# Twenty-four conditioning columns of the first attention layer made on TensorE, and a third raw weight buffer

## The chip, the cores and the metric

The kernel runs on one core of a Trainium2 chip. The metric is device time of one execution in microseconds (us). The engines are TensorE (PE in the rows, PEld for its weight loads), VectorE (DVE), ScalarE (ACT), GpSimd (POOL) and SyncE (SP, which here only issues transfers).

## The reference, cut to what matters

Two transformer layers over 512 tokens of width 1024, in float32. Each layer first makes six conditioning vectors of 1024 values from a vector `c`, uses three of them around the attention and three around the MLP:

```python
c_act = jax.nn.silu(c)
for l in range(DEPTH):                       # DEPTH = 2
    ada = c_act @ ada_w[l] + ada_b[l]        # 1024 x 6144 weights for each layer
    sh1, sc1, g1, sh2, sc2, g2 = jnp.split(ada, 6, axis=-1)
    h = modulate(x, sh1, sc1)                # x * (1 + sc1) + sh1
    y = even_mixer(h, ...) if l % 2 == 0 else diff_mixer(h, ...)
    x = layer_norm(ALPHA * x + (1.0 + g1) * y, ln_g[l, 0], ln_b[l, 0])
    h = modulate(x, sh2, sc2)
    y = sq_relu_mlp(h, mlp_w1[l], mlp_w2[l]) # square(relu(h @ w1)) @ w2, inner width 4096
    x = layer_norm(ALPHA * x + (1.0 + g2) * y, ln_g[l, 1], ln_b[l, 1])
```

`even_mixer` projects `h` once and feeds two attentions: NSA (compressed, selected and windowed keys, 8 heads) and DSA (an indexer scores the keys, the 256 best of each query are kept, 8 heads). Their joined output goes through one output projection.

## The kernel before

**Columns.** The 6144 conditioning values of a layer are 48 columns of 128 (`adac[:, l, m]`). In layer 0, columns 0 to 15 are the shift and scale ahead of the attention, 16 to 23 (`ada2`) the gate `g1`, 24 to 39 (`adaE`) the shift and scale ahead of the MLP, and 40 to 47 the gate `g2`. Each column needs 512 KB of weights. There are two ways to make one:

- on VectorE, GpSimd and ScalarE: the weights lie with one output value per partition, and are multiplied with `cact`, a row of 1024 numbers that stands in every partition. Columns 0 to 15, and three of the others (the table `ax`), take one VectorE instruction that multiplies and sums (L250). The other 21 of columns 16 to 39 take a GpSimd multiplication in place (L247) and a ScalarE pass that sums (L248). `ada_bias` (L407) then adds the bias to eight columns at a time.
- on TensorE, two columns at a time (`ada_pair`, L416): eight matmuls of the raw weights against the vector `ccol` (L422) into a PSUM bank, a ScalarE copy (L425), two small matmuls (L427) that turn the result into two columns, and a VectorE add that takes the bias along (L428). Columns 40 to 47 of layer 0 and all 48 of layer 1 are made so. Of a pair, the first raw buffer stays occupied (`held`) until the matmuls of the pair have read both.

**Stream.** All weights come in one list in program order, by the queue of SP, into raw buffers of 512 KB (`issue`, L134). `process` then prepares each in list order: a column, or a split of a weight chunk into a high part (`hi`, ScalarE cast, L265) and a low part (`lo`, a subtraction on VectorE or GpSimd, L266), which TensorE takes in three matmuls a product (L350 to L352). The output weights (`eo`) are also multiplied by a gate row (`grow`, L262). Two raw buffers stand for the whole kernel; four "early" ones are taken only at the start and up to the NSA, four others only in the tails and MLPs.

**Order.** In `even`, a start phase makes columns 0 to 15 and the first eight weight chunks. Then come input projections (`iq`, `ks`, `kw` and others, L350 to L352), the indexer's scores (L504, L505, the same lines as all scores) with L1159 to L1164 behind them, and the latent keys (L1095 to L1113: an RMS norm, whose L384 to L398 are a square root made by VectorE, and transposes). `n0` is the first chunk of the query projections. The table `ord` sets the order of the loads there; `a` is a column of `ada2`. In the NSA units that follow, `st.pump(2)` takes up to two items from the stream in each; the `adaE` columns and the chunks `eo` are among them, and the gate row is made once `ada2` is done (`gate_row`). The DSA units (about 240 to 370 us) take in the last columns and `eo4` to `eo7`. `gtile` (L537) loads a bias tile, on SP's queue as the weights are.

All engines run their instructions in the order written; the code's order on each engine comes from a scheduler.

Of the kernel before, what the change touches and what calls it, by code (L numbers as in the profile page):

```python
# [9 lines left out]
F32 = mybir.dt.float32  # L10
F32R = mybir.dt.float32r
I32 = mybir.dt.int32
AF = mybir.ActivationFunctionType
ALU = mybir.AluOpType
# [14 lines left out]
def f32(ap):  # L29
# [4 lines left out]
PLAN = {'se': ((0, 1, 0, 0, 1, 0, 0), (0, 1, 1, 0, 0, 1, 0)),  # L34
 'sl': ((1, 1, 0, 1, 0, 1, 0), (1, 0, 0, 0, 0, 0, 0)),
 'ax': ((0, 19), (0, 36), (0, 38)),
 'sc': ('eo2', 'eo3', 'eo4', 'eo5', 'eo7', 'oo5', 'z018'),
 'lo': {'n0': 0,
        'dq2': 1,
        'dq3': 0,  # L40
        'dq0': 1,
        'qk70': 0,
# [28 lines left out]
 'fz': (1, 2, 3, 0, 4, 5),  # L71
 'ord': ('iq', 'a', 'ks', 'n0', 'a', 'kw', 'a', 'a', 'a', 'a', 'kc', 'vc', 0, 'a', 1, 2, 3, 'n1', 4, 5, 'a', 6, 7,
         'n2', 'n3'),
# [33 lines left out]
class Stream:  # L107
# [130 lines left out]
    def prepare(self, it):  # L238
        k, nc = self.k, self.k.nc
        n = it.n  # L240
        raw = it.raw[0][:, :n]
        if it.ada is not None:
            l, m = it.ada
            if not k.ada_pe(l, m):
                acc = k.adac[:, l, m:m + 1]
                if bool(16 <= m < 48) != ((l, m) in PLAN["ax"]):
                    nc.gpsimd.tensor_tensor(out=raw, in0=raw, in1=k.cact, op=ALU.mult)  # L247
                    nc.scalar.activation(out=raw, in_=raw, func=AF.Copy, scale=0.5, accum_out=acc)  # L248
                else:
                    nc.vector.scalar_tensor_tensor(out=raw, in0=raw, scalar=0.5, in1=k.cact, op0=ALU.mult,  # L250
                                                   op1=ALU.mult, accum_out=acc)
            elif m % 2:
                k.ada_pair(l, m - 1, self.held.raw[0], raw)
# [73 lines left out]
class Trunk:  # L327
# [76 lines left out]

    def ada_bias(self, l, sp):
        sl = slice(8 * sp, 8 * sp + 8)
        self.nc.vector.tensor_add(out=self.adac[:, l, sl], in0=self.adac[:, l, sl], in1=self.adab[:, l, sl])  # L407

    def ada_pe(self, l, m):

        return l > 0 or m >= 40

    def ada_src(self, l, m):
        return self.a["ada_p"][8 + m if l else m - 40] if self.ada_pe(l, m) else self.a["ada_w"][m]

# [127 lines left out]
    def start(self):  # L543
        nc, a, C = self.nc, self.a, self.C

        c, t = self.cond, self.s4()
        self.cact = C.tile([128, 1024], F32, name="cact")
        self.one = C.tile([128, 1], F32, name="one")
# [488 lines left out]
    def even(self):  # L1037
        nc, a, sm, R, B, st, I = self.nc, self.a, self.sm, self.R, self.B, self.st, self.I
# [36 lines left out]
        iq = []  # L1075
# [246 lines left out]
        for slot in range(end):  # L1322
# [36 lines left out]
            if n >= 2 and (0, 0) not in self.gate and (I["ada2", 7].done or n == 14):  # L1359
                st.get(I["ada2", 7])  # L1360
                self.ada_bias(0, 2)
                self.gate_row(0, 0)
# [109 lines left out]
        for m in (3, 4):  # L1472
            st.get(I["adaE", 8 * m + 7])
            self.ada_bias(0, m)
        return od, [I["eo", k] for k in range(4, 8)]
# [341 lines left out]
    def run(self):  # L1817
        tc = self.tc
        with tc.tile_pool(name="c", bufs=1) as self.C, tc.tile_pool(name="sm", bufs=1) as self.sm, \
# [3 lines left out]
            st = self.st  # L1823
            for s in range(2):
                st.raws.append((self.W.tile([128, 1024], F32, name=f"raw{s}"), 1 << 30))
# [34 lines left out]
def layout(i):  # L1860
    c = np.ascontiguousarray
    i = {k: np.asarray(v) for k, v in i.items()}
    f = {}
# [9 lines left out]
    f["cT"] = c(i["c"].reshape(8, 128).T)  # L1873
    f["ada_w"] = c(i["ada_w"][0, :, :5120].reshape(1024, 40, 128).transpose(1, 2, 0))
    p = i["ada_w"].reshape(2, 2, 4, 128, 24, 256).transpose(0, 4, 1, 3, 2, 5).reshape(96, 128, 1024)
    f["ada_p"] = c(p[40:])
    f["ada_b"] = c(i["ada_b"].reshape(2, 48, 128).transpose(2, 0, 1))
# [52 lines left out]
```

## Time and profile before

| | |
|---|---|
| time before, median of 3 runs | 1440.21 us (1439.06 to 1440.84) |
| profiled execution, its own time | 1441.48 us |
| its span, first to last instruction | 1439.4 us |
| mean granted TensorE clock | 0.968 |
| TensorE busy | 1338.4 us, 93% |
| VectorE busy | 1141.7 us, 79% |
| ScalarE busy | 659.8 us, 46% |
| GpSimd busy | 579.8 us, 40% |

The shares are means over stages with different limits: the start and even attention (0 to some 370 us), the first MLP, the second attention and the second MLP. TensorE's busy time counts a matmul from its start to a modelled end, so that matmuls that follow each other at some distance also look busy without a gap. The granted clock is 1.00 at 2.4 GHz and 0.50 at 1.2 GHz.

### The profile page before, as it was taken

The numbers are of one execution on the slowest core, as the hardware profiler recorded it, in microseconds if no ns is written. First come the engines' busy times: TensorE is split into PE (matmuls) and PEld (weight loads), VectorE is DVE, ScalarE is ACT, GpSimd is POOL, SyncE is SP. The second block draws the span as 40 slices with busy tenths as digits, with TensorE's granted clock in tenths as the row PEclk, the third lists the DMA queues.
The fourth block names the chain that finished last, engine by engine and source line by source line (L and its number), as shares of the span: only waits on it lengthen the run. The fifth ranks groups of instructions, "written<-read, shape, count | busy, mean of one in ns | idle before, by whom it ended". The sixth has DMA issues, their size and how long they took to land.

```text
span 1439.4 us, 22546 instructions
## 1 busy us (share of the span) xinstructions
PE 1338.4 (93%) x8286; PEld 1123.1 (78%) x8286; DVE 1141.7 (79%) x2186; ACT 659.8 (46%) x1412; POOL 579.8 (40%) x432
## 2 busy tenths in 40 slices
PE   6979799998899999999999799999979899999985
PEld 4868676676589888888887687887769789999974
DVE  7778979667569778877789925788976997888898
ACT  3555465746365423333332536776565443333321
POOL 1423577626432444444453721124164533122234
PEclk9989999899999999999999999999989999999997
DMA  9834323313731554544542442332450233323311
GB/s 353 288 116 142 116 89 118 119 58 118 263 117 46 175 191 162 183 169 161 191 161 94 144 164 88 103 103 76 152 163 6 91 100 118 106 72 117 117 59 59
DMA packets 58657, 189.52 MB, mean 132 GB/s; under 512 B 7794, under 2 KB 8498, under 8 KB 58548
## 3 DMA queue, kind: packets, MB, share of 16 engines
q1 hardware_dynamic: 55840, 184.67, 38.0%
q10 hardware_dynamic: 2708, 3.42, 0.7%
q8 instruction: 65, 1.06, 0.3%
q14 instruction: 44, 0.36, 0.1%
HBM read 178.42 MB, written 9.64 MB: 131 GB/s over the span
## 4 chain that ended last, share of the span: by engine, by line
PE 70%; DVE 19%; DMA 4%; issue 3%; ACT 2%; POOL 1%; DVEq 0%; SPq 0%; ACTq 0%; POOLq 0%
PE ps_mm L350 9%; PE ps_mm L351 9%; PE ps_mm L352 9%; PE ps_o L350 4%; PE ps_o L351 4%; PE ps_o L352 4%; PE ps_s L351 3%; PE ps_s L350 3%; PE ps_s L352 3%; PE ps_t L350 2%; PE ps_t L352 2%; PE ps_t L351 2%; PE ps_t L1486 2%; PE ps_s L504 2%; DVE u L738 2%
## 5 line engine op out<-in xcount | busy, mean ns | idle before, releaser
L350 PE MATMUL ps_mm<-hT,b 128*128 128x256 f32 (+1 forms) x560 | 188.9, 339 | 16.9 <-ACT b L265 13.2
L351 PE MATMUL ps_mm<-hT,b 128*128 128x256 f32 (+1 forms) x560 | 188.5, 337 | 5.2 <-DVE hT L724 5.1
L352 PE MATMUL ps_mm<-hT,b 128*128 128x256 f32 (+1 forms) x560 | 187.8, 336 | 1.8 <-DVE b L220 1.8
L350 PEld LDWEIGHTS ps_mm<-hT,b 128*128 128x128 f32 x560 | 107.6, 192 | 31.9 <-ACT b L265 13.2
L351 PEld LDWEIGHTS ps_mm<-hT,b 128*128 128x128 f32 x560 | 107.8, 193 | 17.8 <-DVE hT L724 5.6
L220 POOL TENSOR_TENSOR b<-s,b 128x512 fp32r<-128x512 f32 x33 | 46.6, 1415 | 184.6 <-ACT b L219 181.2
L517 ACT ACTIVATE z<-z,st 128x128 f32<-128x128 f32 (+3 forms) x160 | 89.3, 559 | 67.2 <-DVE st L514 61.3
L903 POOL TENSOR_TENSOR ot<-z,ot 128x512 fp32r<-128x512 f32 x39 | 61.3, 1573 | 142.0 <-ACT ot L902 128.4
L352 PEld LDWEIGHTS ps_mm<-hT,b 128*128 128x128 f32 x560 | 107.5, 192 | 11.4 <-DVE b L220 2.0
L350 PE MATMUL ps_o<-b,ot 128*128 128x512 f32 x251 | 101.2, 403 | 3.9 <-ACT b L265 2.2
L351 PE MATMUL ps_o<-b,ot 128*128 128x512 f32 x251 | 99.5, 397 | 3.0 <-DVE b L266 3.0
L738 DVE TENSOR_TENSOR u<-ps_o,u 128x512 f32<-128x512 f32 x121 | 82.4, 681 | 21.6 <-PE ps_o L352 21.2
L352 PE MATMUL ps_o<-b,ot 128*128 128x512 f32 x251 | 98.8, 394 | 0.0
L514 DVE CUSTOM_DVE_ANT_0 z<-ps_s,g 128x128 f32<-128x128 f32 (+3 forms) x160 | 75.0, 484 | 25.8 <-PE ps_s L505 23.6
L265 ACT CAST b<-raw 128x1024 fp32r<-128x1024 f32 (+1 forms) x62 | 64.5, 1043 | 65.9 <-issue 16.7
L266 DVE TENSOR_TENSOR b<-s,b 128x1024 fp32r<-128x1024 f32 x47 | 70.4, 1501 | 18.3 <-ACT b L265 17.9
L265 ACT CAST b<-s 128x1024 fp32r<-128x1024 f32 x47 | 49.1, 1049 | 77.6 <-DMA s<-mlp_w 18.9
L266 DVE TENSOR_TENSOR b<-raw,b 128x1024 fp32r<-128x1024 f32 (+1 forms) x42 | 56.7, 1349 | 33.1 <-ACT b L265 32.9
L350 PE MATMUL ps_s<-b,ot 128*128 128x512 f32 x181 | 72.4, 400 | 0.0
L738 DVE TENSOR_TENSOR u<-ps_s,u 128x512 f32<-128x512 f32 x87 | 59.3, 682 | 15.9 <-PE ps_s L352 15.6
L351 PE MATMUL ps_s<-b,ot 128*128 128x512 f32 x181 | 71.7, 396 | 0.0
L352 PE MATMUL ps_s<-b,ot 128*128 128x512 f32 x181 | 71.4, 394 | 0.0
(472 smaller groups left out, 4244.1 us busy)
## 6 DMA issues: line engine op xcount, KB each, us to landing
s<-mlp_w SPq DMA_DIRECT2D x55, 512.0 KB
s<-ada_p SPq DMA_DIRECT2D x39, 512.0 KB
s<-mlp_wp SPq DMA_DIRECT2D x33, 512.0 KB
raw<-ada_w SPq DMA_DIRECT2D x23, 512.0 KB
raw<-mlp_w SPq DMA_DIRECT2D x21, 512.0 KB
raw<-mlp_wp SPq DMA_DIRECT2D x19, 512.0 KB
early<-ada_w SPq DMA_DIRECT2D x17, 512.0 KB
raw<-ada_p SPq DMA_DIRECT2D x17, 512.0 KB
```

The lines of the kernel that those rows point to most:

```text
L220: (nc.gpsimd if PLAN["sl"][it.l][n] else nc.vector).tensor_tensor(out=lo, in0=src, in1=f32(hi), op=ALU.subtract)
L265: nc.scalar.copy(out=hi.cols(c.start, w), in_=raw[:, c])
L266: getattr(nc, ("vector", "gpsimd")[PLAN["lo"][it.name]] if it.name in PLAN["lo"] else k.lo_engine).tensor_sub(out=lo.cols(c.start, w), in0 ...
L350: mm(ps, lhsT=l[0], rhs=r[0], start=start, stop=False)
L351: mm(ps, lhsT=l[0], rhs=r[1], start=False, stop=False)
L352: mm(ps, lhsT=l[1], rhs=r[0], start=False, stop=stop)
L504: mm(ps, lhsT=q[:, qs], rhs=k[0][:, ks], start=start, stop=False)
L514: i = nc.vector.tensor_tensor_reduce(out=z[:, :w], in0=ps, in1=bias, scale=-1.0, scalar=3e38, op0=ALU.add, op1=ALU.min, accum_out=st[:, m: ...
L517: j = nc.scalar.activation(out=z[:, :w], in_=z[:, :w], func=AF.Exp, scale=-1.0, bias=st[:, m:m + 1], accum_out=st[:, 2 + m:3 + m])
L738: self.nc.vector.tensor_add(out=u[:, sl], in0=ps, in1=u[:, sl])
L903: (nc.gpsimd if PLAN["hl"][l][f % 2] else nc.vector).tensor_tensor(out=hl[:, c0:c1], in0=r[:, c0:c1], in1=f32(hh[:, c0:c1]), op=ALU.subtract)
L1486: self.nc.tensor.transpose(t[:, 128 * j:128 * j + 128], z[:, 128 * j:128 * j + 128], self.ident)
```

## The change

All 24 columns 16 to 39 of layer 0 are made by `ada_pair`, so that L247, L248, the table `ax` and `ada_bias` go. The weights of these columns come in the layout of the pairs (`ada_p`); 512 KB a column as before. The row `cact`, which only columns 0 to 15 need now, shares its room with the gate row (`grow`), and a third raw buffer for the whole kernel takes the room that this gives. The table `ord` has `a` at other places: `iq`, then two columns, then `ks` and `n0`, where `iq`, one column, `ks`, `n0` and one column stood.

```diff
- 'ax': ((0, 19), (0, 36), (0, 38)),
...
- 'ord': ('iq', 'a', 'ks', 'n0', 'a', 'kw', 'a', 'a', 'a', 'a', 'kc', 'vc', 0, 'a', 1, 2, 3, 'n1', 4, 5, 'a', 6, 7,
+ 'ord': ('iq', 'a', 'a', 'ks', 'n0', 'kw', 'a', 'a', 'a', 'a', 'kc', 'vc', 0, 'a', 'a', 1, 2, 3, 'n1', 4, 5, 6, 7,
          'n2', 'n3'),
...
             if not k.ada_pe(l, m):
-                acc = k.adac[:, l, m:m + 1]
-                if bool(16 <= m < 48) != ((l, m) in PLAN["ax"]):
-                    nc.gpsimd.tensor_tensor(out=raw, in0=raw, in1=k.cact, op=ALU.mult)
-                    nc.scalar.activation(out=raw, in_=raw, func=AF.Copy, scale=0.5, accum_out=acc)
-                else:
-                    nc.vector.scalar_tensor_tensor(out=raw, in0=raw, scalar=0.5, in1=k.cact, op0=ALU.mult,
-                                                   op1=ALU.mult, accum_out=acc)
+                nc.vector.scalar_tensor_tensor(out=raw, in0=raw, scalar=0.5, in1=k.cact, op0=ALU.mult,
+                                               op1=ALU.mult, accum_out=k.adac[:, l, m:m + 1])
...
-    def ada_bias(self, l, sp):
...
     def ada_pe(self, l, m):

-        return l > 0 or m >= 40
+        return l > 0 or m >= 16
...
-        self.cact = C.tile([128, 1024], F32, name="cact")
+        self.cact = self.B.tile([128, 1024], F32, tag="grow", bufs=1, name="cact")
...
-            for s in range(2):
+            for s in range(3):
                 st.raws.append((self.W.tile([128, 1024], F32, name=f"raw{s}"), 1 << 30))
```

The scheduler places what the change adds. In the changed kernel's code all later lines lie some ten lower: L412, L415, L417 and L418 are the pair's L422, L425, L427 and L428, L344 to L346 are L350 to L352, L494 and L495 are L504 and L505, L1103 is L1113, and L260 is L266.

TensorE before, from the end of the `ks` projection (chunk `b_85`, `b_86`) to the first transposes of the latent keys:

```order
L352 MATMUL ps_mm<-hT,b_86 128x512
L504 MATMUL ps_s<-q,ot 128x512
L505 MATMUL ps_s<-q,ot 128x512
L504 MATMUL ps_s<-q,ot 128x512
L505 MATMUL ps_s<-q,ot 128x512
L1113 MATMUL ps_t<-ident,ot 128x128 x3
L504 MATMUL ps_s<-q,ot 128x512
L505 MATMUL ps_s<-q,ot 128x512
L1113 MATMUL ps_t<-ident,ot 128x128
```

TensorE of the changed kernel at the same place, where `ks` is chunk `b_86`, `b_87`; one pair lies ahead of `ks`, behind `iq`:

```order
L412 MATMUL ps_mm<-raw_75,ccol 32x256 x4
L412 MATMUL ps_mm<-raw_76,ccol 32x256 x4
L344 MATMUL ps_mm<-hT,b_86 128x512
L345 MATMUL ps_mm<-hT,b_86 128x512
L346 MATMUL ps_mm<-hT,b_87 128x512
L1103 MATMUL ps_t<-ident,ot 128x128 x4
L417 MATMUL ps_mm<-sel,z 128x1 x2
L494 MATMUL ps_s<-q,ot 128x512
L495 MATMUL ps_s<-q,ot 128x512
L412 MATMUL ps_mm<-raw_77,ccol 32x256 x4
L412 MATMUL ps_mm<-early,ccol 32x256 x4
L417 MATMUL ps_mm<-sel,z 128x1 x2
```

A second pair stands inside `ks` and a third behind one more score, both ahead of `n0`; a fourth follows `n0`. The remaining eight lie in the NSA and DSA units.

GpSimd before, from its first column to the splits of `kc` and `vc`:

```order
L247 TENSOR_TENSOR early<-early,cact 128x1024
L266 TENSOR_TENSOR b_84<-early,b_83 128x1024
L247 TENSOR_TENSOR early<-early,cact 128x1024
L266 TENSOR_TENSOR b_80<-early,b_79 128x1024
L247 TENSOR_TENSOR raw_75<-raw_75,cact 128x1024
L247 TENSOR_TENSOR early<-early,cact 128x1024 x2
L266 TENSOR_TENSOR b_84<-raw_76,b_83 128x1024
L266 TENSOR_TENSOR b_82<-raw_75,b_81 128x1024
L247 TENSOR_TENSOR early<-early,cact 128x1024
```

GpSimd of the changed kernel there:

```order
L260 TENSOR_TENSOR b_85<-early,b_84 128x1024
L260 TENSOR_TENSOR b_81<-early,b_80 128x1024
L260 TENSOR_TENSOR b_83<-early,b_82 128x1024
L260 TENSOR_TENSOR b_85<-raw_75,b_84 128x1024
L1542 MEMSET ot 128x256
L260 TENSOR_TENSOR b_87<-raw_77,b_86 128x1024
```

The column multiplications are gone and the splits now stand one behind the other.

SP's queue before, at the end of the columns (the loads of the last two `eo` chunks are the rows with `ev_out` behind a `g`):

```order
L134 DMA raw_75<-ev_out 128x1024
L134 DMA raw_76<-ada_w 128x1024
L134 DMA raw_76<-ev_out 128x1024
L1371 DMA u<-x 128x1024
L537 DMA g<-bvec 128x1x512 x3
L134 DMA raw_76<-ev_out 128x1024
L537 DMA g<-bvec 128x1x512
L134 DMA raw_75<-ev_out 128x1024
```

SP's queue of the changed kernel there:

```order
L133 DMA raw_77<-ev_out 128x1024
L1360 DMA u<-x 128x1024
L133 DMA raw_76<-ada_p 128x1024
L133 DMA raw_76<-ev_out 128x1024
L133 DMA raw_75<-ev_out 128x1024
L527 DMA g<-bvec 128x1x512 x4
L133 DMA raw_76<-mlp_w 128x1024
L133 DMA raw_75<-mlp_w 128x1024
L133 DMA raw_77<-ev_out 128x1024
```

Two `ev_out` loads now stand ahead of four bias tiles, where three bias tiles stood ahead of the second last; the last one now follows the bias tiles and two loads of MLP weights.

## Rows read from the trace of the kernel before

**Rows 1.** Page, busy us (share of the span) and number of instructions, of each engine.
```profile
PE 1338.4 (93%) x8286; PEld 1123.1 (78%) x8286; DVE 1141.7 (79%) x2186; ACT 659.8 (46%) x1412; POOL 579.8 (40%) x432
```

**Rows 2.** Busy time by 20 us: TensorE, weight loads, DVE, ACT, POOL; clock; DMA share; GB/s.
```profile
40.00:60.00 20.00, 20.00 (x98) 18.08 (x97) 15.33 (x26) 9.98 (x14) 5.10 (x2) 1.00 0.88 292
60.00:80.00 20.00, 12.40 (x55) 9.99 (x54) 17.23 (x28) 12.36 (x34) 15.12 (x6) 0.87 0.53 189
...
220.00:240.00 20.00, 19.57 (x123) 14.37 (x124) 19.73 (x62) 12.68 (x33) 16.19 (x13) 1.00 0.36 119
240.00:260.00 20.00, 18.09 (x105) 13.38 (x103) 14.75 (x47) 11.70 (x33) 15.69 (x14) 0.74 0.36 97
260.00:280.00 20.00, 18.44 (x110) 11.78 (x110) 13.62 (x36) 15.62 (x37) 14.57 (x15) 0.82 0.46 154
```

**Rows 3.** TensorE's waits from 60 to 340 us: total, times, longest.
```profile
PE ps_s L504 <- DVE st L514: 10.0, 4, 4.0
PE ps_t L1113 <- DVE ot L1106: 7.6, 1, 7.6
PE ps_mm L350 <- DVE ot L473: 2.0, 1, 2.0
```

**Rows 4.** DVE in order of time, 66 to 80 us: start, us, line.
```profile
66.94 3.09 DVE L250 SCALAR_TENSOR_TENSOR raw<-raw,cact 128x1024 f32<-128x1024 f32 x1 [0.19 <-DMA raw<-ada_w]
...
69.95 2.35 DVE L1102 TENSOR_SCALAR ss<-ss 128x4 f32<-128x4 f32 x1
...
72.33 2.31 DVE L384 TENSOR_SCALAR yi<-ss 128x4 int32<-128x4 int32 x1
...
75.22 1.74 DVE L391 TENSOR_TENSOR t<-yi 128x4 f32<-128x4 f32 x1
76.99 0.16 DVE L392 TENSOR_TENSOR t<-t,ss 128x4 f32<-128x4 f32 x1
```

**Rows 5.** POOL in order of time, 66 to 77 us.
```profile
66.53 2.41 POOL L247 TENSOR_TENSOR raw<-raw,cact 128x1024 f32<-128x1024 f32 x1
68.89 5.72 POOL L247 TENSOR_TENSOR early<-early,cact 128x1024 f32<-128x1024 f32 x2
74.59 2.35 POOL L266 TENSOR_TENSOR b<-raw,b 128x1024 fp32r<-128x1024 f32 x1
```

**Rows 6.** Line L247: duration in ns min/median/max, and what POOL waited for ahead of it.
```profile
L247 POOL TENSOR_TENSOR raw<-raw,cact x16: 2352/2390/2544, 66.5 to 290.9; 128x1024 f32<-128x1024 f32 x16
L247 POOL TENSOR_TENSOR early<-early,cact x5: 2377/2405/3379, 47.2 to 89.4; 128x1024 f32<-128x1024 f32 x5
...
  DMA early<-ada_w: 34.2, 3
  DMA raw<-ada_w: 5.4, 6
```

**Rows 7.** Chain that ended last: two pairs made back to back on TensorE.
```profile
384.17 1.86 PE ps_mm L422 x32
386.03 1.10 PE ps_mm L427 x8
```

**Rows 8.** Line L425: the ACT copy of a pair that has a "mm" bank.
```profile
L425 ACT COPY z<-ps_mm x4: 365/372/372, 379.0 to 386.1; 128x256 f32<-128x256 f32 x4
```

**Rows 9.** Busy time and clock of 84 to 88 us, columns as in Rows 2.
```profile
84.00:88.00 4.00, 3.67 (x11) 2.88 (x12) 2.38 (x4) 3.12 (x6) 1.70 (x1) 0.65 0.88 315
```

**Rows 10.** DVE in order of time, at 210 us.
```profile
210.72 2.24 DVE L1243 TENSOR_SCALAR cst<-cst 128x4 f32<-128x4 f32 x1
```

**Rows 11.** DVE in order of time, at 242 us.
```profile
242.25 2.33 DVE L407 TENSOR_TENSOR adac<-adac,adab 128x8 f32<-128x8 f32 x1
```

**Rows 12.** SP, which issues the loads: its waits from 0 to 340 us.
```profile
SPq L537 <- DVE st L514: 35.1, 5, 21.5
```

**Rows 13.** DVE in order of time, at 332 us.
```profile
331.92 1.97 DVE L262 TENSOR_TENSOR raw<-raw,grow 128x1024 f32<-128x1024 f32 x1 [1.58 <-DMA raw<-ev_out]
```

**Rows 14.** Chain that ended last, 600 to 1440 us: a transfer in it.
```profile
1028.90 5.90 DMA s<-mlp_w
```

More of the change, by code (lines that the diff above doesn't have):

```diff
@@ L403, in ada_items @@
         return self.st.items[-1]
-    def ada_bias(self, l, sp):
-        sl = slice(8 * sp, 8 * sp + 8)
-        self.nc.vector.tensor_add(out=self.adac[:, l, sl], in0=self.adac[:, l, sl], in1=self.adab[:, l, sl])
     def ada_pe(self, l, m):
-        return l > 0 or m >= 40
+        return l > 0 or m >= 16
     def ada_src(self, l, m):
-        return self.a["ada_p"][8 + m if l else m - 40] if self.ada_pe(l, m) else self.a["ada_w"][m]
+        return self.a["ada_p"][32 + m if l else m - 16] if self.ada_pe(l, m) else self.a["ada_w"][m]
     def ada_pair(self, l, m, r0, r1):
@@ L1360, in even @@
                 st.get(I["ada2", 7])
-                self.ada_bias(0, 2)
                 self.gate_row(0, 0)
@@ L1473, in even @@
             st.get(I["adaE", 8 * m + 7])
-            self.ada_bias(0, m)
         return od, [I["eo", k] for k in range(4, 8)]
@@ L1873, in layout @@
     f["cT"] = c(i["c"].reshape(8, 128).T)
-    f["ada_w"] = c(i["ada_w"][0, :, :5120].reshape(1024, 40, 128).transpose(1, 2, 0))
+    f["ada_w"] = c(i["ada_w"][0, :, :2048].reshape(1024, 16, 128).transpose(1, 2, 0))
     p = i["ada_w"].reshape(2, 2, 4, 128, 24, 256).transpose(0, 4, 1, 3, 2, 5).reshape(96, 128, 1024)
-    f["ada_p"] = c(p[40:])
+    f["ada_p"] = c(p[16:])
     f["ada_b"] = c(i["ada_b"].reshape(2, 48, 128).transpose(2, 0, 1))
```

## The prediction

> **What bounds the kernel now.** I read the page first, for the engines' shares; the reader is to see that TensorE is busy 93% of the span, but its weight loads only 78% [rows 1]. Then the table by 20 us, for where there is room. From 40 to 60 us weight loads fill 18.1 of 20 us, which is how a dense stretch looks here; from 220 to 240 us TensorE looks just as busy, with 14.4 us of weight loads, while VectorE is busy 19.7 us [rows 2]. So in the NSA units TensorE is handed its work late, by VectorE above all, and a busy TensorE there is not a full one. Third, TensorE's own waits before the MLP: VectorE ends the long ones, 7.6 us for the latent keys, 2.0 us for the query split, 10.0 us for the scores [rows 3]. Last, VectorE and GpSimd in order of time around 70 us, for why the 7.6 us come about. VectorE takes 2.35, 2.31 and 1.74 us for three operations on 128x4 numbers, where the next of that size takes 0.16 us [rows 4]; the last two end when a GpSimd instruction over 128x1024 numbers does, at 74.6 and 76.9 us, and the first ends amid the two that take 5.72 us together [rows 5]. A small VectorE instruction stands still while one of GpSimd's runs; that is how L247 reaches the path.
>
> The Trainium skill (SBUF — State Buffer, Who interferes with whom) says that GpSimd shares one pair of ports with VectorE and that this is an exclusive lock. The trace agrees with the standing still.
>
> **Removed.** It takes away 21 multiplications of 2.4 us on GpSimd [rows 6], some 50 us, and as many ScalarE passes behind them; neither engine is what TensorE waits for much, so alone this is worth nothing. It counts through VectorE, and through what I put a price on here.
>
> At 66 to 90 us: L250 there (3.09 us) becomes TensorE's work, and L1102 and L384 lose 2.19 and 2.15 us, since L247 held them; together 7.4 of the 7.6 us of the wait. L391 stays held by a split (L266, which stays). The 2.0 us behind it: half goes. The clock was granted 0.65 over 84 to 88 us [rows 9], behind these waits, that is, part of the stretch ran at 1.2 GHz: 4 x 0.35 = 1.4 us come back. Sum -7.4 - 1.0 - 1.4 = -9.8 us. All of it and the second wait too would be -11; nothing, if the splits on GpSimd, which now stand one behind the other, hold the same VectorE instructions.
>
> At 120 to 300 us: Five more VectorE instructions are held by L247, the longest 2.24 us at 210 us [rows 10] against some 0.16; I take 6 us for the five. `ada_bias` goes too, one of which was held 2.33 us at 242 us [rows 11]; the same split (L266) that held it may then hold the next small instruction. Of these 8.3 us I count half, -4, as VectorE is full from 220 to 240 us but not behind 240 [rows 2]; ends 0 and -8.3. Behind 242 us TensorE waits and the clock falls: 0.74 and 0.82 mean over 240 to 280 us [rows 2], that is 20 x 0.26 + 20 x 0.18 = 8.8 us of full-speed work lost. If one of the two falls goes, about a third of that returns: -3; ends 0 and -8.8.
>
> **Added.** Twelve pairs on TensorE. Two pairs back to back take 1.86 us for the large matmuls and 1.10 us for the small [rows 7], so a pair is 0.93 + 0.55 = 1.48 us, twelve 17.8 us. The ScalarE copy between them is 0.37 us [rows 8]; by the rows of order in the section on the change, other work mostly stands between a pair's halves on TensorE, so I add nothing for it, except where the small matmuls stand right behind the large ones (the third pair): some 0.5 us, inside the rounding of what follows.
>
> Four pairs lie at 60 to 110 us, where the wait is taken away: +5.9. The front sum is -9.8 + 5.9 = **-4**. Ends: -8, if half the pairs fit into what is left of the waits; +6, if nothing is gained.
>
> Eight lie in the NSA and DSA units: 11.8 us. The stretch 220 to 240 us has weight loads for 14.4 of 20 us against 18.1 where TensorE is dense [rows 2], a fifth of free room, some 3.7 us every 20 us; eight pairs over some 120 us (190 to 310) have room for all by this, but not where they happen to stand. I take half: +5.9, ends 0 and 11.8.
>
> A pair also waits, on TensorE, for its weights, which GpSimd waited for before: 5.4 us in 6 times for `raw` [rows 6]. Behind a waiting pair all of TensorE's queue stands, the scores and with them VectorE's softmax. The loads come sooner, since TensorE gives the buffers back at once and a third one is there, but a pair needs two and holds one meanwhile: +1.5, ends 0 and 5.4. The middle sum is -4 - 3 + 5.9 + 1.5 = **+0.4**.
>
> **Moved.** The load of `eo6` stood on SP's queue behind three bias tiles, and SP waited up to 21.5 us for VectorE to give such a tile's room [rows 12]; VectorE then waited 1.58 us for the weights [rows 13]. In the new order two `ev_out` loads pass the bias tiles: **-1.5**; ends 0, and -2, as little more than the wait can go. The last `ev_out` now stands behind two loads of MLP weights, which needs time on the transfers only; I count nothing for it, since VectorE was through with the chunk before it when the old one landed.
>
> **The third raw buffer later.** In the MLPs and the second attention six buffers become seven. The chain has few transfers there, one of 5.90 us [rows 14]; a load that starts one buffer sooner would shorten such pieces: **-1**, ends 0 and -5. The room of `cact` costs nothing: column 15 is long made when the gate row needs it.
>
> **Sum.** -4 + 0.4 - 1.5 - 1 = -6.1 us against the profiled execution's own 1441.5 us, whose span is 1439.4 with some 2 us around it. This execution stands 1.3 us above the median of 1440.2, so I forecast 1440.2 - 6.1 = **1434 us** (own range 1428 to 1438).
>
> **Rivals.**
>
> *A: TensorE is full, and all twelve pairs are paid.* For: 93% busy [rows 1]. Against: the weight loads of 78%, and VectorE at 19.7 of 20 us. Then the middle has no room and VectorE's relief is worth nothing: 11.8 + 1.5 there, the front -4, the tail and the buffer -2.5, sum +6.8: 1447 us. It decides from the point at which more than three quarters of the middle's pairs are paid and none of the clock comes back. The Trainium skill (Perfetto Trace Analysis, Identifying the Most-Contended Engine) says to optimize the most contended engine first, which speaks against adding to TensorE; it also says that weight loads, not matmul busy time, measure its room. By the first half the sum would be that of this rival, by the second that of the forecast.
>
> *B: TensorE waits for the columns' weights.* For: GpSimd waited 34.2 us in 3 times and 5.4 us in 6 [rows 6] for just these, and SP's queue stands up to 21.5 us behind a bias tile [rows 12]; a pair that stands on TensorE before its weights have come would stop all. Against: TensorE reaches a pair later than GpSimd reached its column, and the buffers come back sooner. Price: 0.9 us (5.4 / 6) for each of twelve pairs is 10.8 us, against the 1.5 in my sum: +9.3, and 3 of clock that isn't recovered: -6.1 + 12.3 = +6.2; with one more fall of the clock (3 us) it is +9.2: 1449 us. It decides from about 0.6 us of such a wait per pair.
>
> *C: the gain goes into other waits.* The splits, back to back on GpSimd, hold VectorE at 66 to 80 us as L247 did, and in the middle the 10.0 us of waits for the softmax [rows 3], which L247 has little part in, stay. Then the front is 0 (the pairs fill the wait, nothing is saved), the rest -2: 1438 to 1441, 1440 us.
>
> *D: the clock stays up.* If both falls of 240 to 280 us go, 8.8 instead of 3 us return, and the pairs, which fill what were gaps, are absorbed whole (5.9 more): 1434 - 11.7 = 1422 us. Against: the four waits for the softmax [rows 3] have little to do with L247, and a wait is what the clock fell behind at 242 us.
>
> **How the numbers follow.** Forecast 0.45, A 0.13, B 0.12, C 0.17, D 0.13. 0.2% is 2.9 us, about what a measurement here can tell from no change. Faster: forecast and D, 0.58; same: C, 0.17; slower: A and B, 0.25. The range runs from 1421 (D) to 1448 (A whole, B in part), which leaves out some 0.15 to 0.2.
>
> **What the profile after would show.** Right: no wait of over 2 us on TensorE from 70 to 90 us, L1092 (the old L1102) at 0.16 us, more than 18 us of TensorE in 60 to 80 us, and a clock of 1.00 there; pairs of about 1.5 us; weight loads above 15 us in 220 to 240 us; no wait of VectorE for `ev_out` at 330 us. The stage boundaries then come earlier: the scores by some 4 us at 110 us, the first MLP by 5 us at 375 us. Wrong: rows of the pairs' L412 that wait for a transfer (B), a clock that falls elsewhere, or small VectorE instructions of 2 us and more behind L260 in the front (C). A start of the first MLP that is later than before, with weight loads as few as now, would make the whole sum wrong.

## The result, and the profile after

The change made the kernel slower: 1452.23 us (median of 5 runs, 1447.30 to 1454.12) against 1440.21 us, ratio 1.0077 with a 95% interval of 1.0053 to 1.0100. In a second series, beside the last experiments, it took 1453.71 us, ratio 1.0087 (1.0060 to 1.0115). The profiled execution is one of the shorter: 1449.07 us. Runs of one kernel scatter here: the kernel before took 1431 to 1450 us over all series. So a single profile is good for where things stand, and medians for what they cost.

The page of the changed kernel, its busy times:

```profile
PE 1354.2 (94%) x8526; PEld 1127.4 (78%) x8526; DVE 1130.4 (78%) x2189; ACT 640.4 (44%) x1382; POOL 526.9 (36%) x411
```

GpSimd lost 53 us of work and ScalarE 19; TensorE gained 16 [rows 1]. The stretches that the prediction spoke of, first by the table of busy times (columns as in [rows 2]), then by TensorE's waits from 60 to 340 us:

```profile
60.00:80.00 20.00, 17.28 (x69) 11.75 (x68) 15.39 (x30) 10.68 (x32) 4.77 (x2) 0.74 0.48 164
220.00:240.00 20.00, 18.79 (x140) 13.49 (x136) 19.31 (x70) 11.21 (x32) 7.66 (x11) 1.00 0.25 79
240.00:260.00 20.00, 17.95 (x104) 13.47 (x104) 13.14 (x49) 7.09 (x25) 7.21 (x12) 0.66 0.25 86
260.00:280.00 20.00, 20.00 (x155) 13.27 (x153) 11.29 (x32) 10.47 (x27) 7.54 (x9) 1.00 0.27 93
```

```profile
PE ps_s L494 <- DVE st L504: 3.9, 3, 1.5
PE ps_mm L417 <- ACT z L415: 2.3, 2, 1.8
PE ps_mm L344 <- ACT k L479: 1.9, 2, 1.0
PE ps_s L494 <- DVE ot L463: 1.8, 2, 1.4
PE ps_s L494 <- ACT z L1198: 1.0, 1, 1.0
```

The waits did shrink, from 7.6 and 10.0 us to 3.9 and less [rows 3], and TensorE looks busier. But in 60 to 80 us the granted clock is 0.74 on average, lower than the 0.87 of before (0.83 in a second profile of the changed kernel, e16 below), and the weight loads of 220 to 280 us are hardly more than they were (40.2 against 39.5 us), though four pairs were added there [rows 2]. VectorE, in order of time in the front:

```profile
59.82 1.22 DVE L260 TENSOR_TENSOR b<-raw,b 128x1024 fp32r<-128x1024 f32 x1
...
62.52 2.32 DVE L260 TENSOR_TENSOR b<-early,b 128x1024 fp32r<-128x1024 f32 x1
...
74.42 0.17 DVE L1092 TENSOR_SCALAR ss<-ss 128x4 f32<-128x4 f32 x1
```

and GpSimd and TensorE there:

```profile
61.35 2.41 POOL L260 TENSOR_TENSOR b<-early,b 128x1024 fp32r<-128x1024 f32 x1 [11.60 <-ACT b L259]
```

```profile
67.78 0.69 PE L494 MATMUL ps_s<-q,ot 128*128 128x512 f32 x1 [1.35 <-DVE ot L463]
...
87.60 0.61 PE L417 MATMUL ps_mm<-sel,z 128*128 128x1 f32 x4 [1.84 <-ACT z L415]
```

L1092 (L1102 before) now takes 0.17 us, as forecast [rows 4]. But another VectorE instruction, a split, takes 2.32 us beside a GpSimd split, where the split ahead of it took 1.22; TensorE's scores wait behind it, and the third pair's small matmuls wait 1.84 us for the ScalarE copy.

Where the kernel stands against the one before, stage by stage. The table is worked out from the profiles: for all instructions whose line occurs equally often in both, the difference of their starts, and of these the median in a window of the time before. Each window is 10 us long and begins at the time in the head, in us. From 210 to 290 us the kernels do the attention units in different orders, so no window is taken there.

| kernel | 110 | 180 | 300 | 366 | 384 | 975 | 1085 |
|---|---|---|---|---|---|---|---|
| changed kernel | +7.5 | +2.6 | +13.1 | +6.8 | +1.8 | +2.4 | +10.0 |
| e16: the changed kernel again | +7.7 | +3.2 | +15.9 | +9.6 | +4.5 | +7.1 | +16.1 |
| e1: third buffer only in layer 1 | +12.1 | +7.9 | +13.3 | +6.9 | +2.1 | +5.1 | +5.5 |
| e2: two buffers | +3.1 | +1.2 | +16.6 | +13.4 | +14.4 | +17.4 | +18.9 |
| e3: old order of loads | -4.7 | -7.8 | +7.3 | +1.0 | -4.2 | -4.2 | +0.5 |
| e5: pairs only for 16 to 23, two buffers | +1.9 | +1.2 | -8.7 | -8.7 | -7.2 | -6.5 | -5.0 |
| e13: no pairs for 24 to 39 | +9.1 | +4.3 | -5.8 | -8.3 | -10.3 | -10.2 | -5.6 |
| e14: the same, two buffers | +3.8 | +2.1 | -5.7 | -8.0 | -6.3 | -5.3 | -5.0 |

One profile a kernel is little: e16 is the same kernel as the first row, and e1 has the same order of TensorE's work up to 380 us, yet their rows differ by up to 6 us. Three places stand out even so: 180 to 366 us, where every kernel without late pairs gains 10 to 13 us and most with them lose, up to 12; 366 to 384 us, where kernels with three buffers gain 2 to 5; and 975 to 1085 us, where those that have three in the second layer lose 5 to 9.

### The profile page after: what moved, and what is told of

Its sections match the earlier page's. It is cut to its first block, busy times and chain, and to the rows that moved or that the text cites. A ratio compares the mean times of both kernels' runs of the same rounds, so it can differ in the third digit from the quotient of the medians.

```text
span 1447.3 us, 22974 instructions
## 1 busy us (share of the span) xinstructions
PE 1354.2 (94%) x8526; PEld 1127.4 (78%) x8526; DVE 1130.4 (78%) x2189; ACT 640.4 (44%) x1382; POOL 526.9 (36%) x411
## 4 chain that ended last, share of the span: by engine, by line
PE 71%; DVE 18%; ACT 3%; issue 3%; DMA 2%; POOL 1%; SPq 0%; DVEq 0%; ACTq 0%; POOLq 0%
PE ps_mm L344 9%; PE ps_mm L345 9%; PE ps_mm L346 9%; PE ps_o L344 4%; PE ps_o L345 4%; PE ps_o L346 4%; PE ps_s L344 3%; PE ps_s L345 3%; PE ps_s L346 3%; PE ps_t L344 2%; PE ps_t L346 2%; PE ps_t L345 2%; DVE b L260 2%; PE ps_t L1474 2%; PE ps_s L494 2%
## 5 line engine op out<-in xcount | busy, mean ns | idle before, releaser
L344 PE MATMUL ps_mm<-hT,b 128*128 128x256 f32 (+1 forms) x560 | 189.7, 341 | 17.9 <-ACT b L259 13.2
L346 PE MATMUL ps_mm<-hT,b 128*128 128x256 f32 (+1 forms) x560 | 188.0, 337 | 1.8 <-DVE b L219 1.8
L344 PEld LDWEIGHTS ps_mm<-hT,b 128*128 128x128 f32 x560 | 107.8, 193 | 34.3 <-ACT b L259 13.2
L346 PEld LDWEIGHTS ps_mm<-hT,b 128*128 128x128 f32 x560 | 107.8, 193 | 11.5 <-DVE b L219 2.0
L259 ACT CAST b<-raw 128x1024 fp32r<-128x1024 f32 (+1 forms) x78 | 81.0, 1045 | 75.5 <-POOL raw L256 17.6
L344 PE MATMUL ps_o<-b,ot 128*128 128x512 f32 x251 | 100.5, 400 | 2.9 <-ACT ot L892 1.5
L260 DVE TENSOR_TENSOR b<-raw,b 128x1024 fp32r<-128x1024 f32 (+1 forms) x55 | 74.2, 1352 | 35.0 <-ACT b L259 34.3
L260 POOL TENSOR_TENSOR b<-raw,b 128x1024 fp32r<-128x1024 f32 x23 | 55.4, 2409 | 124.3 <-ACT b L259 110.5
L504 DVE CUSTOM_DVE_ANT_0 z<-ps_s,g 128x128 f32<-128x128 f32 (+3 forms) x160 | 75.8, 485 | 29.4 <-PE ps_s L495 25.4
L346 PE MATMUL ps_o<-b,ot 128*128 128x512 f32 x251 | 98.2, 391 | 0.0
L728 DVE TENSOR_TENSOR u<-ps_o,u 128x512 f32<-128x512 f32 x121 | 82.3, 681 | 16.8 <-PE ps_o L346 16.5
L219 POOL TENSOR_TENSOR b<-raw,b 128x512 fp32r<-128x512 f32 x25 | 34.6, 1385 | 145.8 <-ACT b L218 145.8
L344 PE MATMUL ps_s<-b,ot 128*128 128x512 f32 x181 | 71.6, 396 | 0.1
L346 PE MATMUL ps_s<-b,ot 128*128 128x512 f32 x181 | 70.7, 390 | 0.0
L728 DVE TENSOR_TENSOR u<-ps_s,u 128x512 f32<-128x512 f32 x87 | 59.3, 681 | 12.5 <-PE ps_s L346 12.2
L219 POOL TENSOR_TENSOR b<-s,b 128x512 fp32r<-128x512 f32 x21 | 30.9, 1471 | 102.7 <-ACT b L218 93.5
```

What stands on the lines that cost most here:

```text
L219: (nc.gpsimd if PLAN["sl"][it.l][n] else nc.vector).tensor_tensor(out=lo, in0=src, in1=f32(hi), op=ALU.subtract)
L259: nc.scalar.copy(out=hi.cols(c.start, w), in_=raw[:, c])
L260: getattr(nc, ("vector", "gpsimd")[PLAN["lo"][it.name]] if it.name in PLAN["lo"] else k.lo_engine).tensor_sub(out=lo.cols(c.start, w), in0 ...
L344: mm(ps, lhsT=l[0], rhs=r[0], start=start, stop=False)
L346: mm(ps, lhsT=l[1], rhs=r[0], start=False, stop=stop)
L504: i = nc.vector.tensor_tensor_reduce(out=z[:, :w], in0=ps, in1=bias, scale=-1.0, scalar=3e38, op0=ALU.add, op1=ALU.min, accum_out=st[:, m: ...
```

## The experiments

All but e4, e5 and e6 start from the changed kernel. "Late pairs" are those of columns 24 to 39. Every kernel goes through the scheduler anew. Of TensorE's 2066 matmuls outside the pairs in the first 380 us, none stands elsewhere than in the changed kernel in e1 and e16, but 474 do in e15 and 780 to 1540 in e2, e3 and e7 to e14. So the time of an experiment is that of its edit together with the order that it got.

**e1, the third buffer withdrawn at the second layer.**

```diff
-            self.raws = [r for r in self.raws if r[1] > self.issued]
+            self.raws = [r for r in self.raws if r[1] > self.issued and not (len(r) > 2 and self.issued >= self.cut)]
```

> The changed kernel, with the third raw buffer withdrawn from the stream at the first weights of the second layer, so that the second layer loads through the same number of buffers as before the change. Theory T (third buffer): matched instruction by instruction, the changed kernel's profile is 0.8 us behind the kernel before at 415 to 500 us, 2.5 us at 985 us and 10 us from 1060 us on; the 7.5 us of 985 to 1060 us come from the other buffer rotation of the second layer. Then this kernel takes about 1443 us, and its lag stays at 2 to 3 us from 500 us to the end. Rival R (pairs): the twelve pairs on TensorE cost the time, and the lag at 985 to 1060 us comes with any shift of the timing; then this takes 1450 to 1453 us, like the changed kernel.

1448.81 us, ratio 1.0053 (1.0032 to 1.0074), 3.4 us under the changed kernel, with intervals that overlap. The time is nearer to R; but the lag of 975 to 1085 us did go (+0.4 where the changed kernel has +7.6). So the place is right, and it isn't the main cause. SP's loads of the first MLP weights of the second layer, and the wait of TensorE behind them, in the kernel before, the changed kernel and e1:

```profile
1024.31 2.57 SPq L134 DMA_DIRECT2D raw<-mlp_w  x2
```

```profile
1061.81 1.11 PE L713 MATMUL ps_t<-ident,ot 128*128 128x128 f32 x4 [6.92 <-ACT ot L719]
```

```profile
1030.16 1.48 SPq L133 DMA_DIRECT2D s<-mlp_w  x2
```

```profile
1070.66 1.11 PE L703 MATMUL ps_t<-ident,ot 128*128 128x128 f32 x4 [8.96 <-ACT ot L709]
```

```profile
1029.48 2.57 SPq L133 DMA_DIRECT2D raw<-mlp_w  x2
```

```profile
1067.37 1.11 PE L703 MATMUL ps_t<-ident,ot 128*128 128x128 f32 x4 [6.92 <-ACT ot L709]
```

With three buffers the first of these loads goes to another kind of buffer (`s`), the order of work behind it differs, and TensorE waits 8.96 instead of 6.92 us. That is 2.0 of the 7.6 us; from 975 to 1100 us its waits for VectorE's `u` (L728, L738 before) also grow from 2.9 to 5.4 us, and the granted clock over 1040 to 1100 us is 0.83 instead of 0.89. All nine profiles with three buffers in the second layer lose 4.6 to 9.1 us from 975 to 1085 us, the eight others with two lose -0.4 to 1.5.

**e2, two buffers throughout.**

```diff
-            for s in range(3):
+            for s in range(2):
```

> The changed kernel with two raw buffers for the whole kernel instead of three, the columns and the order of loads as changed. T: the loss at 985 to 1060 us goes, but the 6 us that the changed kernel makes good between 372 and 415 us (6.8 behind, then 0.8) go too, as the third buffer is what made them good: about 1447 us. R: the pairs cost the time, and they wait for one buffer more: 1452 us or more. If the third buffer does nothing anywhere, as the changed kernel, 1452 us.

1458.64 us, ratio 1.0108 (1.0083 to 1.0133): worse than T said, and as R said. Its lag at 366 us is +13.4, and nothing comes back behind it. TensorE waits for columns' weights here (waits from 180 to 380 us), and for VectorE at the layer norm, where the kernel before waited 3.46 us and the changed kernel doesn't wait (e2, then the kernel before):

```profile
PE ps_mm L412 <- DMA raw<-ada_p: 4.6, 2, 3.6
```

```profile
386.41 1.09 PE L703 MATMUL ps_t<-ident,ot 128*128 128x128 f32 x4 [5.70 <-DVE ot L690]
```

```profile
372.43 1.94 PE L713 MATMUL ps_t<-ident,ot 128*128 128x128 f32 x8 [3.46 <-DVE ot L700]
```

**e3, the old order of loads.**

```diff
- 'ord': ('iq', 'a', 'a', 'ks', 'n0', 'kw', ..., 0, 'a', 'a', 1, 2, 3, 'n1', 4, 5, 6, 7,
+ 'ord': ('iq', 'a', 'ks', 'n0', 'a', 'kw', ..., 0, 'a', 1, 2, 3, 'n1', 4, 5, 'a', 6, 7,
```

> The changed kernel with the order of loads of the kernel before (one column, then the ks weights, n0, another column). In the changed kernel's profile the ks projection starts about 4 us later than before, behind a pair and scores, and the last scores come 7.5 us later at 113 us. If the place of the second column costs that, the lag at 113 us falls to some 4 us here; T says that this is not what the end hangs on, since the lag is 0.8 us at 415 us anyway: 1450 to 1452 us. R, by which the front's lag comes through to the end: 1448 us.

1446.56 us, ratio 1.0030 (1.0010 to 1.0050): nearest to R's number. At 110 us it stands 12 us ahead of the changed kernel, at 180 us 10, at 300 and 366 us 6, and the medians differ by 5.7: about half of the front's lead comes through. Its profile is the fastest of its 12 runs, 1439.23 us.

**e4, the kernel before with the new order** (the same edit the other way round, on the kernel before).

> The kernel before (columns on GpSimd and ScalarE, two raw buffers) with the changed order of loads alone. T: the ks weights come one load later (512 KB, some 1.3 us), which the start's 7.6 us wait of TensorE partly covers: 1440 to 1442 us. If the order is what makes the front late, the ks projection is 3 to 4 us later here too, and the time 1443 to 1444 us.

1436.06 us, ratio 0.9970 (0.9948 to 0.9992). Neither expectation: the order is worth 4 us to the kernel with columns on GpSimd and two buffers, and costs the one with all pairs and three buffers 6 us (e3). Why it turns its sign stays open.

**e5 and e6, one half of the pairs alone,** on e4, that is with two buffers and the new order.

```diff
-        return l > 0 or m >= 40
+        return l > 0 or 16 <= m < 24 or m >= 40    # e5
+        return l > 0 or m >= 24                    # e6
```

> The kernel before with the changed order of loads and two raw buffers, with only the eight columns 16 to 23 (four pairs, at 60 to 110 us) made on TensorE. Without any of the 12 pairs this kernel took 1436.1 us, with all of them 1458.6 us, so 22.5 us are to be divided. Theory P (the place decides): the front's pairs fill waits, as the prediction had it, and the loss is in the NSA and DSA units: 1436 to 1439 us. Rival Q (each pair costs the same): a third of it, 1443 to 1444 us. Rival F (the front's pairs and their half clock cost it): 1450 us or more.

> The kernel before with the changed order of loads and two raw buffers, with only the sixteen columns 24 to 39 (eight pairs, in the NSA and DSA units) made on TensorE. P: nearly all of the 22.5 us, 1455 to 1458 us. Q: two thirds, 1451 us. F: 1440 to 1444 us.

e5: 1436.14 us, ratio 0.9968 (0.9955 to 0.9982). e6: 1452.87 us, ratio 1.0090 (1.0070 to 1.0109). e5 is P's number; e6 lies between Q's 1451 and P's 1455. So the place decides in the main: against e4's 1436.06 us the four early pairs cost 0.1 us and the eight late ones 16.8, 2.1 us each where a pair's own time is 1.48 [rows 7]. The two halves don't add up, though: both together cost 22.5 us (e2).

**e7, the large matmuls of the 12 pairs twice.**

```diff
-        for k in range(8):
+        for k in list(range(8)) * (2 if l == 0 and m < 40 else 1):
```

> The changed kernel with the eight large matmuls of each of the 12 new pairs made twice into the same bank (the second time from the start, so the sums are the same), with no load, wait or buffer more: 12 x 0.93 = 11.2 us of TensorE's own time are added. If TensorE is full where the pairs stand, and their cost is their own time, 1452 + 11 = 1463 us. If their cost is what waits in order behind and ahead of them (weights, the copy, the bank) and the matmuls themselves lie in free room, 1452 to 1455 us. The prediction's own half: 1457 to 1458 us.

1456.32 us, ratio 1.0115 (1.0095 to 1.0135): 4.1 us for 11.2 us of work, between the second and the third. Taken alone this reads as waits rather than own time. But the clock changed too. Busy times from 200 to 320 us (columns as in [rows 2]) of the changed kernel and of e7:

```profile
200.00:320.00 120.00, 114.32 (x822) 82.36 (x823) 81.11 (x262) 55.93 (x156) 41.49 (x52) 0.94 0.31 102
```

```profile
200.00:320.00 120.00, 115.96 (x944) 78.48 (x940) 72.71 (x247) 53.07 (x149) 40.87 (x53) 1.00 0.30 102
```

A clock of 1.00 instead of 0.94 (0.93 in e16) is 7 to 8 us of full-speed work in 120 us, and the order is another one, so the 4.1 us are not the price of the doubled matmuls alone.

**e8, the old order and e1 together.**

> The changed kernel with two parts taken back together: the old order of loads, and the third raw buffer withdrawn at the second layer. Alone they took it from 1452.2 to 1446.6 and to 1448.8 us. If the two add up, 1443 us; if both act on one thing, 1446 to 1447 us. With all 12 pairs on TensorE and the third buffer in the first layer, under 1440 us would say that the columns on TensorE cost nothing and all was the order and the second layer.

1444.12 us, ratio 1.0028 (1.0008 to 1.0049): the two nearly add up, and still nothing under 1440.

**e9 to e12, the late pairs in another PSUM bank.** In the changed kernel a pair holds one of two "mm" banks until VectorE's add. The third late pair, on TensorE, ScalarE and VectorE:

```profile
233.83 1.07 PE L412 MATMUL ps_mm<-raw,ccol 128*32 128x256 f32 x16
```

```profile
247.43 0.37 ACT L415 COPY z<-ps_mm 128x256 f32<-128x256 f32 x1 [1.35 <-PE ps_t L1249]
```

```profile
249.56 0.15 DVE L418 TENSOR_TENSOR adac<-ps_mm,adab 128x2 f32<-128x2 f32 x1
```

Its matmuls take 1.07 us, the bank is held for 15.9. Meanwhile projections that need such a bank slip in the order.

```diff
-        ps = self.bank(self.ada_tag)
+        ps = self.bank("t" if l == 0 and 24 <= m < 40 else self.ada_tag)    # e9; "o" in e10, "s" in e11; e12: e8 with "t"
```

> The changed kernel, with the eight pairs of columns 24 to 39 in a bank of the transposes' tag ("t") instead of the projections' ("mm"); nothing else. Theory B (bank): in the changed kernel a pair holds one of the two "mm" banks for 4 to 16 us, 75.7 us over the eight, from its first matmul to the add on VectorE, and the query projections, which need such a bank, slip: three of them end behind 81, 121 and 145 of the 160 value products (L1304 before) in TensorE's order, against 64, 81 and 85 in the kernel before. With the other bank they end behind 73, 85 and 92, and most of the 16.8 us that these eight pairs cost with two raw buffers comes back: 1440 to 1444 us. Rival L (loads and TensorE's own time): the bank has no part, 1450 to 1453 us. If the transposes suffer from the held bank as the projections did, 1452 us or more.

> As the run before, with the pairs of columns 24 to 39 in a bank of the value products' tag ("o"). The projections end behind 80, 89 and 92 value products, so B says 1441 to 1446 us, unless the value products, which are many and short, suffer from the held bank; L says 1450 to 1453 us.

> As the two runs before, with the pairs of columns 24 to 39 in a bank of the scores' tag ("s"). The projections end behind 73, 92 and 92 value products; B: 1441 to 1446 us; L: 1450 to 1453 us.

> The changed kernel with three things taken back or mended: the bank of the pairs of columns 24 to 39 ("t"), the old order of loads, and the third raw buffer withdrawn at the second layer. Without the bank the other two gave 1444.1 us. B, if its 8 to 12 us come on top: 1432 to 1436 us, below the kernel before and below both of the kernels of 1436 us; L: 1444 us; if bank and old order act on one thing, 1438 to 1441 us.

1450.31 us (1.0078, 1.0046 to 1.0109), 1446.45 (1.0035, 1.0015 to 1.0055), 1449.08 (1.0055, 1.0032 to 1.0078) and 1441.56 (0.9996, 0.9972 to 1.0019). With "t" the projections stand nearly where they stood before, and the time is 2 us less, within the intervals. So B, that the "mm" bank is the main cause, isn't borne out; that a pair holds some other bank there instead, at a cost of its own, isn't ruled out. The 6 us of "o" are at the edge of what these intervals can tell. e12 has all twelve pairs on TensorE and stands 10.7 us under the changed kernel and 17 under e2: what the pairs cost depends that much on what stands around them.

**e13 and e14, no late pairs at all,** with three and with two buffers. Columns 24 to 39 are zero; their weights are loaded and not used.

```diff
-            elif m % 2:
+            elif m % 2 and not (l == 0 and 24 <= m < 40):
```

> The changed kernel without the pairs of columns 24 to 39 (they are set to zero, their weights are loaded and not used): no engine makes these columns. Theory O (own time): what the eight pairs cost is TensorE's own time, 8 x 1.48 = 11.8 us, paid whole, and freeing GpSimd and VectorE of the columns is worth nothing: 1452.2 - 11.8 = 1440.4 us. Rival W (waits around them): the pairs also cost by what stands behind them, 1433 to 1436 us. Rival H (half, as the prediction had it): 1446 us.

> The same with two raw buffers for the whole kernel; with the eight pairs this took 1458.6 us, with the same columns made on GpSimd and ScalarE 1436.1 us. O: making these columns on GpSimd costs nothing, so that leaving them out gives 1435 to 1437 us; the 22.5 us are then all the pairs', 11.8 of them TensorE's own and about 5 waits for weights that show in the trace. If GpSimd's work did hold VectorE on the path, as the prediction had it (4 us of VectorE and 3 of clock), this takes 1428 to 1431 us.

e13: 1435.63 us, ratio 0.9962 (0.9942 to 0.9982). e14: 1435.79 us, ratio 0.9964 (0.9944 to 0.9984). e13 is W's number, e14 is O's, and the two settle the most. e14 against e5: leaving the columns out is worth 0.3 us, nothing by these intervals, over making them on GpSimd, ScalarE and VectorE. So their relief was worth nothing. e14 against e2, and e13 against the changed kernel: the late pairs cost 22.9 us with two buffers, 16.6 with three. e13 against e14: without late pairs the third buffer is worth nothing. Busy times from 240 to 300 us (columns as in [rows 2]) of the changed kernel, of e13 and of e5:

```profile
240.00:300.00 60.00, 56.49 (x399) 40.29 (x398) 31.60 (x93) 24.26 (x65) 18.64 (x23) 0.89 0.35 117
```

```profile
240.00:300.00 60.00, 56.74 (x387) 42.77 (x386) 41.10 (x124) 33.27 (x87) 21.06 (x26) 0.97 0.29 97
```

```profile
240.00:300.00 60.00, 58.17 (x394) 42.93 (x392) 45.31 (x129) 39.24 (x100) 38.31 (x34) 1.00 0.41 128
```

TensorE looks equally busy in all three. With the late pairs VectorE gets 31.6 us of work, without them 41 to 45: the attention units that feed it come later. The clock is 0.89 with the late pairs (0.91 in e16), 0.97 and 1.00 without. GpSimd has 38.3 us in e5 and 21.1 in e13, and the time is the same.

**e15, thin late pairs,** and **e16, the changed kernel again** beside it. In e15 the late pairs' large matmuls write 16 columns instead of 256, and their small ones take 16 values; the rest of these columns is zero.

```diff
-            mm(ps[32 * j:32 * j + 32, :256], ..., rhs=(r0, r1)[k // 4][:, 256 * j:256 * j + 256],
+            mm(ps[32 * j:32 * j + 32, :w], ..., rhs=(r0, r1)[k // 4][:, 256 * j:256 * j + w],    # w = 16 for late pairs
```

> The changed kernel with the large matmuls of the eight pairs of columns 24 to 39 cut from 256 to 16 output columns, and what follows them cut to 16 values (the rest of these columns is zero); their number, loads, waits, banks and place in the order stay. With the pairs whole 1452.2 us, without them 1435.6 us, so 16.6 us are the pairs'. If that is the time of their large matmuls (8 x 0.93 = 7.4 us, less if the weight loads set their pace) it falls by up to 7: 1445 to 1448 us. If it is what stands around them (order, bank, copy, small matmuls), it stays at 1450 to 1452 us. If the pairs cost by their mere presence in the stream's loads, also 1450 to 1452 us, against which speaks that the loads alone cost nothing.

> The changed kernel itself once more, beside the run with thin pairs on the same chip: 1450 to 1453 us, ratio 1.006 to 1.009.

e15: 1445.76 us, ratio 1.0041 (1.0019 to 1.0063). e16: 1453.71 us, ratio 1.0087 (1.0060 to 1.0115). So 8 us of the late pairs' cost go. TensorE's busy time and weight loads from 200 to 320 us of their large matmuls (L412) and their small ones (L417) in the changed kernel, then of the same two in e15:

```profile
200.00:320.00 120.00, 8.77 (x128) 3.23 (x128) 0.94 0.31 102
200.00:320.00 120.00, 5.35 (x32) 5.27 (x32) 0.94 0.31 102
```

```profile
200.00:320.00 120.00, 3.63 (x128) 2.35 (x128) 0.96 0.33 106
200.00:320.00 120.00, 1.86 (x32) 1.22 (x32) 0.96 0.33 106
```

The large matmuls lost 5.1 us and the small ones, which became thinner too, 3.5: the 8.6 us taken off came back nearly whole. Some 10 us (1445.8 - 1435.6) stay, 5.5 of them the thin matmuls and 4.6 more. The order didn't stay as it was, as the expectation had it (474 of 2066 matmuls moved, none before 217 us), so this is a strong hint and no proof.

## Why the prediction was wrong

**The step that failed** is the middle sum, "-4 - 3 + 5.9 + 1.5 = +0.4". It measured +16.6 us (e13 against the changed kernel; by e14 and e5, making these columns on the old engines costs no more than leaving them out).

- *"I take half: +5.9"*, for eight pairs in the free room that the weight loads seemed to show. Their own time is 11.8 us by the forecast's figures and 14.1 us in the changed kernel's trace; by e13 and e15 it was paid, with 2.5 to 5 us on top. The step from "14.4 us of weight loads in 20" [rows 2] to "3.7 us of room" was the error. My reading is that between loosely spaced matmuls there is time, but those matmuls wait in order for softmax and splits, and what is put ahead of them delays both. VectorE's 31.6 against 41.1 us fit this; no run isolates it.
- *"-4"* for VectorE's relief. GpSimd does hold VectorE [rows 4, 10, 11], and the relief came: from 60 to 310 us, seven VectorE instructions on at most eight numbers a partition take over 1.2 us in the kernel before, 14.8 us together, and two in the changed kernel, 3.7 us. But e14 against e5 gives 0.3 us for the late columns, and e5 against e4 nothing for the early ones, pairs included: the held instructions weren't what TensorE's order hung on.
- *"-3"* for the clock. Of the 8.8 us lost over 240 to 280 us, 2.0 came back (3.6 in e16): the fall of 260 to 280 us went (0.82 to 1.00), that of 240 to 260 us stayed (0.74 to 0.66; 0.74 in e16). The mean of the whole execution rose as well, from 0.968 to 0.975 (0.972 in e16), and the time rose all the same. So the term was about right and the time did not follow it.
- *"+1.5"* for weights that a pair waits for: with two buffers 4.6 us in e2's trace, with three none among the longest waits of the changed kernel. The third buffer was the cure for that.

**The front, "-4"**: right in what it said would shrink, wrong in what follows. The 7.6 us wait went, and yet the stage came 7.5 us later at 110 us, by new waits (1.84 us for a copy that was priced at some 0.5) and the clock's fall (0.74). The pairs are not what makes it late. At 110 us the nine profiles with three buffers and the new order are 7.5 to 12.1 us behind, the five with two buffers and the new order 1.8 to 3.8 (e4 without any pair 3.2), and the three with three buffers and the old order 3.4 to 4.7 us ahead. So the lag goes with the third buffer together with the new order, and the prediction put both at nothing here. The early pairs cost nothing (e5: 0.1 us). That e5, with the new order and the early pairs, measured the forecast's -4 is luck: e4 has the same -4 from the order alone, which was no term of the sum.

**The tail, "-1.5", and the third buffer, "-1"**: VectorE's wait for `ev_out` fell from 1.58 [rows 13] to 0.6 us:

```profile
DVE raw L256 <- DMA raw<-ev_out: 0.6, 1, 0.6
```

From 366 to 384 us kernels with three buffers gain 2 to 5 us, as TensorE has other work at the layer norm. In the second layer they lose 4.6 to 9.1 us by the other turn of the buffers, which I took to be only able to gain. e13 against e14 gives the sum of all that the third buffer does without late pairs: 0.2 us.

**The rivals.** A was the nearest: TensorE is full, 1447 us; the pairs of the middle are paid, as it said, but its front gain is not there and up to 5 us stand on top. B's waits for weights came only with two buffers. C was right that GpSimd's splits hold VectorE in the front (2.32 us for a split of 1.22). D had the whole 8.8 us of clock come back and the pairs absorbed; 2.0 to 3.6 us came, and they were not. The signs named for a wrong sum were there: the first MLP starts later (+1.8 us at 384 us), with weight loads hardly above those of before. Of the two halves of the rule that A quoted (the Trainium skill, Perfetto Trace Analysis, Identifying the Most-Contended Engine), the first, to optimize the most contended engine first, agrees with e13, where taking work off TensorE gave 16.6 us. The second, to judge its headroom by weight loads (the page names MFU, the share of peak FLOPs, beside them), did not hold as it was used here: the changed kernel has 40.3 us of weight loads in 60, and the late pairs were not free there.

**The sum from the runs.** New order and early pairs: 1440.2 to 1436.1 (e5). Late pairs with two buffers: to 1458.6 (e2), that is +22.5, of which some 12 are TensorE's own time by [rows 7], 4.6 waits for weights, and the rest what stands around them. Third buffer: to 1452.2, -6.4, waits and tail gained, front and second layer lost.

**Open.** How the 2.5 to 5 us beyond the pairs' own time divide between the bank, the copy, the clock and the order (e9 to e11 leave up to 6 us for the bank in one of three choices, and 2 in another; the clock of 0.89 to 0.91 against e13's 0.97 over 240 to 300 us is 4 to 5 us of full-speed work). What the late pairs would cost in the best order: the same twelve pairs stand at 1441.6 us in e12 and 1458.6 in e2, and e12 was not run without them. Why doubling the large matmuls (e7) cost only 4.1 us where thinning the late pairs (e15) gave 8; clock and order differ in both. Why the new order gains 4 us with two buffers (e4), though it is 3.2 us late at 110 us.

The best versions with all columns made are e4 and e5, 1436.1 us, some 0.3% under the kernel before: the new order of loads with two buffers and the late columns left on GpSimd and ScalarE. As e13 and e14 show, late columns made by nobody would give no more.

## What to carry to other kernels

Work on an idle engine that nobody waits for can be free. Here, moving it to the engine that all the others feed cost its own time and some more in a stretch whose trace showed only loose spacing (16.6 us for eight pairs), and nothing where that engine stood still for whole microseconds (0.1 us for four). Test the worth of a relief by leaving the work out altogether before it is moved; e14 would have said in one run that there was nothing to gain. A buffer more changes the turn of all later loads, so look for its price in stages far from the change. Where a scheduler orders the work, an experiment changes the order too: compare the orders before a difference is put down to the edit.

## What the runs showed of the hardware that was not expected

Over 240 to 300 us TensorE has 40 us of weight loads in 60 (against 18.1 in 20 where it is dense, [rows 2]), and eight pairs of 1.5 us put there and just around it still cost 16.6 us; doubling the large matmuls of all twelve (e7) then cost 4.1 us for 11.2, with a clock of 1.00 where it had been 0.94. And small VectorE instructions that take 2.2 us instead of 0.16 beside a GpSimd multiplication [rows 10] cost the kernel nothing measurable: 0.3 us between e5, which has 14 such multiplications for the late columns, and e14, which has none.
